# Start addresses of TensorE's operands in a hybrid conformer block: moving tiles and the low halves of the weights shifted within 256 bytes

## The chip, the cores and the metric

The kernel runs on one core of a Trainium2 chip. The metric is the device time of one execution in microseconds (us). TensorE (PE in the profile) multiplies, VectorE (DVE), ScalarE (ACT) and GpSimd (POOL) work on vectors, and SyncE (SP) issues the DMAs. PEld is the row of TensorE's weight loads.

## The reference

Two layers over 256 tokens of width 2048, all in float32. Layer 0 mixes by a convolution branch and a pooling branch, layer 1 by a short gated convolution, and each layer ends in a SwiGLU of width 5632:

```python
for i in range(2):
    h = h + (conv_pool_mixer if i == 0 else short_conv_mixer)(h, ...)
    h = h + swiglu(rms_norm(h, ffn_norm[i]), w_gate[i], w_up[i], w_down[i])
return rms_norm(h, final_norm)

def swiglu(h, w_gate, w_up, w_down):
    return (silu(h @ w_gate) * (h @ w_up)) @ w_down

def short_conv_mixer(x, norm_g, w_in, conv_w, w_out):
    gate_b, gate_c, v = split(rms_norm(x, norm_g) @ w_in, 3)
    return (gate_b * causal_depthwise_conv(gate_c * v, conv_w)) @ w_out
```

The weights are some 390 MB, and each 128x128 block of them is used once, against 256 tokens.

## The kernel before

**Blocks and halves.** All weights lie in one array `wall` as a sequence of 128x128 blocks, in the order in which TensorE uses them. `fetch` (lines 100 to 104) brings them in units of 16 blocks (1 MB). `prepare` (106 to 122) takes a piece of 8 blocks: ScalarE rounds it to float32r into the tile `hi` (line 114), and VectorE, or GpSimd for some early pieces, writes the remainder `w - hi` to the tile `lo` (line 121). There are 6 buffers of each, and pieces are prepared 4 ahead.

**Moving operands.** The activations are split in the same way. Per 128 features, a moving tile holds 256 columns of the high part and then 256 columns of the low part, together 2048 bytes in each partition. There are four such tiles. `xs` (line 210) is the normed input of every stage, `cat` (373) the output of the two branches of the first mixer, `y` (541) the gated product of a SwiGLU half, and `z` (566) the gated convolution of the second mixer.

**Three products for one block.** `product` (161 to 168) has two forms. The narrow one, used in the first mixer and for the last 22 blocks, issues three matmuls of 256 columns: `hi` by the high part (166), `hi` by the low part (167), `lo` by the high part (168). The wide one, used everywhere else, issues two: `hi` by all 512 columns (163), and `lo` by the 256 columns of the high part (164). Each matmul brings its own load of a 128x128 weight tile. In the trace this load begins together with the matmul ahead of the one that it belongs to. Columns of one matmul are therefore read while the next weights are read.

**Stages, in order.** The first mixer (called m0) runs from the start to about 260 us. The first SwiGLU follows, in two halves: gate and up by `xs` (704 blocks), and down by `y` (352 blocks). Then comes the second mixer (m1: 768 blocks by `xs`, 256 by `z`) and the second SwiGLU, like the first. The order on each engine is set when the program is built. Matmuls in a stage follow block by block; VectorE's and ScalarE's work is placed between them by `tick`, by dependencies and by the free buffers.

**Addresses.** The program gives every tile a fixed start in the partition. Buffers of `hi` and `lo` are 4096 bytes apart, blocks in a piece 512 bytes apart, and chunks of a moving tile 2048 bytes apart. So a tile keeps one start modulo 256 for all its blocks. In the kernel before, `hi`, `lo` and `xs` all start at 64 modulo 256, `cat` at 96, and `y` and `z` at 160.

Of the kernel before, what the change touches and what calls it, by code (L numbers as in the profile page):

```python
# [12 lines left out]
F32R = mybir.dt.float32r  # L13
# [4 lines left out]
P = 128  # L18
T = 256
D = 2048  # L20
NC = D // P
DC = 1024
NA = DC // P
FF = 5632
NF = FF // P
NH = NF // 2
# [38 lines left out]
UNIT_AT = [sum(UNITS[:u]) for u in range(len(UNITS))]  # L65

PIECE = 8
PIECES = [(u, o, min(PIECE, n - o)) for u, n in enumerate(UNITS) for o in range(0, n, PIECE)]

LOOK = 4  # L70
AHEAD = 1

WARM = 9

KEEP = 8

POOL_SPLIT = range(96, 24 * NC + 16 + 7 * NC + 8)

# [6 lines left out]
def block_kernel(ctx: ExitStack, tc: tile.TileContext, xT: bass.AP, xtok: bass.AP, vec: bass.AP, wall: bass.AP, out: bass.AP):  # L85
    nc = tc.nc
    const = ctx.enter_context(tc.tile_pool(name="const", bufs=1))
    act = ctx.enter_context(tc.tile_pool(name="act", bufs=1))
    wst = ctx.enter_context(tc.tile_pool(name="wst", bufs=4))
    whl = ctx.enter_context(tc.tile_pool(name="whl", bufs=6))  # L90
# [9 lines left out]
    def fetch(u):  # L100
        if u < len(UNITS) and u not in loaded:
            n, off = UNITS[u], UNIT_AT[u] * P * P
            loaded[u] = w = wst.tile([P, 16 * P], F32, name="w")
            nc.sync.dma_start(w[:, : n * P], wall[off : off + n * P * P].rearrange("(p f) -> p f", p=P))  # L104

    def prepare(i):
        if i >= len(PIECES) or i in ready:
            return
        u, o, n = PIECES[i]
        fetch(u)  # L110
        w = loaded[u][:, o * P : (o + n) * P]
        hi = whl.tile([P, PIECE * P], F32R, name="hi")
        lo = whl.tile([P, PIECE * P], F32R, name="lo")
        nc.scalar.copy(hi[:, : n * P], w)  # L114
        engine = nc.vector
        if UNIT_AT[u] + o in POOL_SPLIT:
            if relief:
                relief.pop()
            else:
                engine = nc.gpsimd  # L120
        engine.tensor_tensor(out=lo[:, : n * P], in0=w, in1=hi[:, : n * P], op=ALU.subtract)  # L121
        ready[i] = (hi, lo)

    def next_block():
        b, i = cursor
        at = UNIT_AT[PIECES[i][0]] + PIECES[i][1]
        if b == at + PIECES[i][2]:
            ready.pop(i)
            i, at = i + 1, b
        for j in range(i, i + LOOK + 1):  # L130
            prepare(j)
        if i + LOOK < len(PIECES):
            for u in range(PIECES[i + LOOK][0] + 1, PIECES[i + LOOK][0] + AHEAD + 1):
                fetch(u)
        cursor[:] = [b + 1, i]
        hi, lo = ready[i]
        o = (b - at) * P
        return hi[:, o : o + P], lo[:, o : o + P]
# [8 lines left out]
    def tick():  # L147
        for name, q in queues.items():
            credit[name] = credit[name] + 1.0 if q else 0.0
            while q and credit[name] >= PACE[q[0][0]]:  # L150
                cost, step = q.popleft()
                credit[name] -= PACE[cost]
                step()
# [7 lines left out]
    def product(acc, hi, lo, x, first, last, wide):  # L161
        if wide:
            nc.tensor.matmul(acc, hi, x, start=first, stop=False, skip_group_check=True)  # L163
            nc.tensor.matmul(acc[:, T:], lo, x[:, :T], start=False, stop=last, skip_group_check=True)  # L164
        else:
            nc.tensor.matmul(acc[:, :T], hi, x[:, :T], start=first, stop=False)  # L166
            nc.tensor.matmul(acc[:, :T], hi, x[:, T:], start=False, stop=False)  # L167
            nc.tensor.matmul(acc[:, :T], lo, x[:, :T], start=False, stop=last)  # L168

    def matmul_chunks(xs, ks, n=1, wide=False, behind=None):  # L170


        accs = [ps.tile([P, 2 * T], F32, name="acc") for _ in range(n)]
        for i, k in enumerate(ks):
            first, last = i == 0, i == len(ks) - 1
            for acc in accs:
                hi, lo = next_block()
                product(acc, hi, lo, xs[:, k, :], first, last, wide)
                tick()
            if behind is not None:  # L180
                behind(k)
        return accs
# [10 lines left out]
    def split(dst, src, scale=None):  # L193

        if scale is None:
            nc.scalar.copy(dst[:, :T], src)
            nc.vector.tensor_tensor(out=dst[:, T:], in0=src, in1=dst[:, :T], op=ALU.subtract)
        else:
            nc.scalar.activation(dst[:, :T], src, AF.Copy, scale=scale)
            nc.vector.scalar_tensor_tensor(out=dst[:, T:], in0=src, scalar=scale, in1=dst[:, :T], op0=ALU.mult, op1=ALU.subtract)  # L200
# [4 lines left out]
    def col(name, i):  # L205
        return v[:, VECS[name] + i : VECS[name] + i + 1]

    identity = v[:, VECS["identity"] :]
    h = act.tile([P, NC, T], F32, name="h")
    xs = act.tile([P, NC, 2 * T], F32R, name="xs")  # L210
    ones = const.tile([P, P], F32, name="ones")
    nc.gpsimd.memset(ones, 1.0)

# [14 lines left out]
    def rsqrt_of(*totals, scale, halves=False, st=None):  # L228
# [9 lines left out]
        if halves:  # L238

            idle = ps.tile([P, P], F32, name="idle", tag="acc")  # L240
            with tc.issue_after(mm.ins):
                for _ in range(KEEP):
                    nc.tensor.matmul(idle, ones, ones, start=True, stop=True)  # L243
# [27 lines left out]
    class Norm:  # L271


        def __init__(self, gain, final=False):
            self.gain, self.final = gain, final
            self.sums = []

        def add(self, c):
# [6 lines left out]

        def scale(self, c):
            if not self.final:
                split(xs[:, c, :], h[:, c, :], col(self.gain, c))

        def square(self, c):  # L290
            if c == 0:
# [37 lines left out]
        return s  # L329


    norm = Norm("mix_norm_e")
    nc.sync.dma_start(v[:, :NC], vec[:, :NC])

    def load(at, n):
# [30 lines left out]
    every = range(NC)  # L366
    with tc.tile_pool(name="m0", bufs=1) as m0, tc.tile_pool(name="ps_side", bufs=2, space=PSUM) as ps_side:
# [1 line left out]
        a_in = m0.tile([P, NA, pad + T], F32, name="a_in")  # L369
        nc.gpsimd.memset(a_in[:, :, :pad], 0.0)  # L370
        conv = m0.tile([P, NA, T], F32, name="conv")
        cat = m0.tile([P, NA, 2 * T], F32R, name="cat")
        total = m0.tile([P, 2, T], F32, name="total")

        sides, prods, state = {}, {}, {}
# [156 lines left out]

        project(xs, POOL_CHUNKS)
        drain()
        norm = Norm("ffn_norm0")
        project(cat, range(NA), norm)

    def swiglu(norm, following):
        with tc.tile_pool(name="ffn", bufs=1) as fp:
            phase[0] = fp  # L540
            y = fp.tile([P, NH, 2 * T], F32R, name="y")
            r = None
            for half in range(2):
                for f in range(NH):
                    (acc_g,) = matmul_chunks(xs, every, wide=True)
                    (acc_u,) = matmul_chunks(xs, every, wide=True)
                    if r is None:
                        r = norm.rstd()
                    gate = scaled(acc_g, r, "gate", True)
                    up = scaled(acc_u, r, "val", True)  # L550
                    nc.scalar.activation(gate, gate, AF.Silu)
                    nc.vector.tensor_tensor(out=up, in0=up, in1=gate, op=ALU.mult)
                    split(y[:, f, :], up)
                project(y, range(NH), following if half else None, wide=True, narrow_end=half and following.final)
# [1 line left out]
    x0.close()  # L556


    after = Norm("mix_norm_o")
    swiglu(norm, after)  # L560


    norm = Norm("ffn_norm1")
    with tc.tile_pool(name="m1", bufs=1) as m1:
        phase[0] = m1
        z = m1.tile([P, NC, 2 * T], F32R, name="z")
        pad = SW - 1
        r = None
        for c in range(NC):
            (acc_c,) = matmul_chunks(xs, every, wide=True)  # L570
            (acc_v,) = matmul_chunks(xs, every, wide=True)
            if r is None:
                r = after.rstd()
            cg = scaled(acc_c, r, "gate", True)
            vv = scaled(acc_v, r, "val", True)
            cv = m1.tile([P, pad + T], F32, name="cv", bufs=2)
            nc.gpsimd.memset(cv[:, :pad], 0.0)
            nc.vector.tensor_tensor(out=cv[:, pad:], in0=cg, in1=vv, op=ALU.mult)
            wc = VECS["conv_w_o"] + c * SW
            co = m1.tile([P, T], F32, name="co", bufs=2)  # L580
            nc.vector.tensor_scalar(out=co, in0=cv[:, :T], scalar1=v[:, wc : wc + 1], scalar2=None, op0=ALU.mult)
            for k in range(1, SW):
                nc.vector.scalar_tensor_tensor(out=co, in0=cv[:, k : k + T], scalar=v[:, wc + k : wc + k + 1], in1=co, op0=ALU.mult, op1=ALU.add)
            (acc_b,) = matmul_chunks(xs, every, wide=True)
            bg = scaled(acc_b, r, "pv", True)
            nc.vector.tensor_tensor(out=bg, in0=bg, in1=co, op=ALU.mult)
            split(z[:, c, :], bg)
        project(z, every, norm, wide=True)


    last = Norm("final_norm", final=True)
    swiglu(norm, last)
    halves = rsqrt_of(*last.sums, scale=1.0 / D, halves=True)
    with tc.tile_pool(name="fin", bufs=1) as fin:

# [90 lines left out]
```

## Time and profile before

| | us |
|---|---|
| median of 3 runs (lowest, highest) | 2105.78 (2104.46, 2109.65) |
| the profiled execution | 2103.73 |
| its span, first to last instruction | 2102.0 |
| bytes read from HBM | 391.39 MB, 187 GB/s over the span |

The page gives each engine's busy time, the chain of work that ended last, and groups of instructions by source line with the mean duration of one. How fast matmuls follow each other isn't in these groups, since they overlap in the pipeline: the mean of one wide `hi` matmul is 391 ns, though they and their `lo` matmuls take turns. That rate comes from another view, the instructions of one source line in a window of time: it prints how many there are and when the first and the last began. The time between the two, divided by the count less one, is the time from one block to the next.

### The profile page before, as it was taken

Reading aid. Unit: us, or ns where it says so; the run is one execution under the profiler, and the core shown is the slowest. Engines: PE = TensorE matmul, PEld = TensorE weight load, DVE = VectorE, ACT = ScalarE, POOL = GpSimd, SP = SyncE. Lnnn points to the kernel's source line nnn. Section 1 sums busy time; section 2 is a strip of 40 time slices with the busy share of each in tenths; the row PEclk is TensorE's granted clock in tenths of the full one; section 3 lists DMA queues with packets and bytes.
Section 4 is the critical chain, followed back from the end, with each engine's and each line's share of the span. In section 5 each row is a group of like instructions: output and inputs, shape, how many; then the busy total and the mean of one; then the engine's idle time right before and its main releaser. Section 6 shows DMA issues by size and latency. Waiting matters only on the chain.

```text
span 2102.0 us, 31608 instructions
## 1 busy us (share of the span) xinstructions
PE 2079.1 (99%) x12584; PEld 1855.8 (88%) x12584; DVE 1383.4 (66%) x1979; ACT 1060.9 (50%) x1571; POOL 200.6 (10%) x180
## 2 busy tenths in 40 slices
PE   8999999999999999999999999999999999999998
PEld 8999988888888888888888888888888888888887
DVE  6888866666556666666777777666666556666654
ACT  7776654444444444454444445554444444444453
POOL 3985200000000000011000001100000000000011
PEclk9999999999999999999999999999999999999999
DMA  8554455555555555555555555555555555555551
GB/s 326 187 191 168 158 184 197 183 198 182 194 185 188 193 187 194 183 196 182 183 198 182 198 183 193 180 189 198 183 196 184 189 192 183 198 182 199 182 192 68
DMA packets 56884, 395.53 MB, mean 188 GB/s; under 512 B 6432, under 2 KB 7200, under 8 KB 9760
## 3 DMA queue, kind: packets, MB, share of 16 engines
q1 hardware_dynamic: 56736, 393.52, 52.4%
q8 instruction: 98, 1.61, 0.3%
q14 instruction: 50, 0.41, 0.1%
HBM read 391.39 MB, written 2.10 MB: 187 GB/s over the span
## 4 chain that ended last, share of the span: by engine, by line
PE 98%; DMA 1%; DVE 1%; ACT 0%; SPq 0%; issue 0%; DVEq 0%; ACTq 0%
PE acc L163 57%; PE acc L164 30%; PE acc L166 4%; PE acc L168 4%; PE acc L167 4%; DMA rows<-in_xtok 0%; DMA h<-in_xT 0%; DVE res L603 0%; ACT hi L114 0%; PE st L237 0%; PE st L268 0%; DVE lo L121 0%; SPq L104 0%; ACT conv L475 0%; PE idle L243 0%
## 5 line engine op out<-in xcount | busy, mean ns | idle before, releaser
L114 ACT CAST hi<-w 128x1024 fp32r<-128x1024 f32 (+1 forms) x740 | 776.1, 1050 | 975.3 <-PE acc L163 621.0
L121 DVE TENSOR_TENSOR lo<-w,hi 128x1024 fp32r<-128x1024 f32 (+1 forms) x691 | 845.2, 1224 | 639.5 <-ACT hi L114 635.3
L163 PE MATMUL acc<-xs,hi 128*128 128x512 f32 x3584 | 1243.3, 391 | 0.0
L164 PE MATMUL acc<-xs,lo 128*128 128x256 f32 x3584 | 1004.7, 280 | 0.0
L163 PEld LDWEIGHTS acc<-xs,hi 128*128 128x128 f32 x3584 | 670.4, 187 | 146.2
L164 PEld LDWEIGHTS acc<-xs,lo 128*128 128x128 f32 x3584 | 678.1, 189 | 0.1
L163 PE MATMUL acc<-y,hi 128*128 128x512 f32 x1386 | 485.2, 393 | 0.0
L164 PE MATMUL acc<-y,lo 128*128 128x256 f32 x1386 | 386.4, 279 | 0.0
L163 PEld LDWEIGHTS acc<-y,hi 128*128 128x128 f32 x1386 | 259.4, 187 | 61.7
L164 PEld LDWEIGHTS acc<-y,lo 128*128 128x128 f32 x1386 | 259.9, 187 | 0.4
L298 POOL TENSOR_TENSOR sumsq<-sumsq,sq 128x256 f32<-128x256 f32 x56 | 58.8, 1050 | 1599.1 <-ACT sq L296 1599.1
L166 PE MATMUL acc<-xs,hi 128*128 128x256 f32 x512 | 144.0, 284 | 5.2 <-ACT hi L114 4.2
L167 PE MATMUL acc<-xs,hi 128*128 128x256 f32 x512 | 143.6, 283 | 0.0
L168 PE MATMUL acc<-xs,lo 128*128 128x256 f32 x512 | 141.3, 284 | 0.1
L121 POOL TENSOR_TENSOR lo<-w,hi 128x1024 fp32r<-128x1024 f32 x49 | 118.7, 2441 | 43.1 <-PE acc L167 34.3
L166 PEld LDWEIGHTS acc<-xs,hi 128*128 128x128 f32 x512 | 98.1, 192 | 6.2 <-ACT hi L114 5.0
L167 PEld LDWEIGHTS acc<-xs,hi 128*128 128x128 f32 x512 | 98.2, 192 | 0.0
L168 PEld LDWEIGHTS acc<-xs,lo 128*128 128x128 f32 x512 | 96.5, 192 | 0.5 <-DVE lo L121 0.5
L163 PE MATMUL acc<-z,hi 128*128 128x512 f32 x256 | 89.6, 393 | 0.0
L188 ACT COPY cross<-acc 128x256 f32<-128x256 f32 x224 | 80.6, 360 | 0.0
L164 PE MATMUL acc<-z,lo 128*128 128x256 f32 x256 | 71.3, 279 | 0.0
L318 DVE TENSOR_TENSOR h<-acc,h 128x256 f32<-128x256 f32 x112 | 47.2, 423 | 18.9 <-PE acc L168 13.2
(134 smaller groups left out, 1198.6 us busy)
## 6 DMA issues: line engine op xcount, KB each, us to landing
w<-in_wall SPq DMA_DIRECT2D x365, 1024.0 KB, 4.8
w<-in_wall SPq DMA_DIRECT2D x7, 512.0 KB, 7.7
rows<-in_xtok SPq DMA_DIRECT2D x2, 1024.0 KB, 7.9
h<-in_xT SPq DMA_DIRECT2D x7, 256.0 KB, 7.3
out<-res SPq DMA_DIRECT2D x2, 512.0 KB, 2.8
out<-res SPq DMA_DIRECT2D x2, 384.0 KB, 2.8
v<-in_vec SPq DMA_DIRECT2D x1, 260.0 KB, 6.7
h<-in_xT SPq DMA_DIRECT2D x2, 128.0 KB, 2.3
```

The lines of the kernel that those rows point to most:

```text
L114: nc.scalar.copy(hi[:, : n * P], w)
L121: engine.tensor_tensor(out=lo[:, : n * P], in0=w, in1=hi[:, : n * P], op=ALU.subtract)
L163: nc.tensor.matmul(acc, hi, x, start=first, stop=False, skip_group_check=True)
L164: nc.tensor.matmul(acc[:, T:], lo, x[:, :T], start=False, stop=last, skip_group_check=True)
L166: nc.tensor.matmul(acc[:, :T], hi, x[:, :T], start=first, stop=False)
L167: nc.tensor.matmul(acc[:, :T], hi, x[:, T:], start=False, stop=False)
L168: nc.tensor.matmul(acc[:, :T], lo, x[:, :T], start=False, stop=last)
L188: nc.scalar.copy(t, acc[:, T:])
L298: nc.gpsimd.tensor_tensor(out=self.sums[0], in0=self.sums[0], in1=sq, op=ALU.add)
L318: nc.vector.tensor_tensor(out=h[:, n, :], in0=acc[:, :T], in1=h[:, n, :], op=ALU.add)
```

## The change

No instruction is added, removed or moved: on each of the five engines, the instructions stand in the same order with the same shapes as before. What differs is where the operands lie.

- `xs` gets 256 bytes more room, and each norm writes and reads it through a view that begins `at` bytes in: 32 for m0, 160 for all later stages. `y` and `z` get 128 bytes more, and begin 64 bytes in. `cat` stays where it was (offset 0).
- Each `lo` buffer gets 512 bytes more, and its view begins 0 bytes in for m0, then 32, 64, 96, 128 and 192 bytes in, from part to part. The shift grows at the block numbers in `LO_AT`. The `hi` buffers keep their place modulo 256.

In the table, "by" is the moving operand's start less the weights' start, modulo 256 bytes.

| part (blocks) | moving | before: by `hi` / by `lo` | after: by `hi` / by `lo` |
|---|---|---|---|
| m0, narrow (512) | xs | 0 / 0 | 32 / 32 |
| m0, narrow (144) | cat | 32 / 32 | 32 / 32 |
| first SwiGLU, half 1 (704, 352) | xs, y | 0 / 0, 96 / 96 | 160 / 128 |
| first SwiGLU, half 2 (704, 352) | xs, y | 0 / 0, 96 / 96 | 160 / 96 |
| m1 (768, 256) | xs, z | 0 / 0, 96 / 96 | 160 / 64 |
| second SwiGLU, half 1 (704, 352) | xs, y | 0 / 0, 96 / 96 | 160 / 32 |
| second SwiGLU, half 2 (704, 330 and 22 narrow) | xs, y | 0 / 0, 96 / 96 | 160 / 224 |

The core of the diff:

```diff
+_m0, _ffn = 24 * NC + 16 + NC * NC, 3 * NH * NC
+LO_AT = {_m0: 32, _m0 + _ffn: 32, _m0 + 2 * _ffn: 32, _m0 + 2 * _ffn + 64 * NC: 32, _m0 + 3 * _ffn + 64 * NC: 64}
+XS_M0 = 32
+XS_F0 = 160
+XS_M1 = 160
+XS_F1 = 160
+Y_F0 = 64
+Y_F1 = 64
+Z_M1 = 64
+CAT = 0
...
-        lo = whl.tile([P, PIECE * P], F32R, name="lo")
+        lo = whl.tile([P, PIECE * P + 128], F32R, name="lo")
+        at = sum(LO_AT[b] for b in LO_AT if b <= UNIT_AT[u] + o) // 4
+        lo = lo[:, at : at + PIECE * P]
...
-    xs = act.tile([P, NC, 2 * T], F32R, name="xs")
+    xs_room = act.tile([P, NC * 2 * T + 64], F32R, name="xs")
+    def moving(room, at, n):
+        return room[:, at // 4 : at // 4 + n * 2 * T].rearrange("p (c t) -> p c t", c=n)
...
-        def __init__(self, gain, final=False):
+        def __init__(self, gain, at=0, final=False):
             self.gain, self.final = gain, final
+            self.xs = moving(xs_room, at, NC)
...
-                split(xs[:, c, :], h[:, c, :], col(self.gain, c))
+                split(self.xs[:, c, :], h[:, c, :], col(self.gain, c))
...
-        cat = m0.tile([P, NA, 2 * T], F32R, name="cat")
+        cat = moving(m0.tile([P, NA * 2 * T + 32], F32R, name="cat"), CAT, NA)
...
-            y = fp.tile([P, NH, 2 * T], F32R, name="y")
+            y = moving(fp.tile([P, NH * 2 * T + 32], F32R, name="y"), at, NH)
...
-        z = m1.tile([P, NC, 2 * T], F32R, name="z")
+        z = moving(m1.tile([P, NC * 2 * T + 32], F32R, name="z"), Z_M1, NC)
```

More of the change, by code (lines that the diff above doesn't have):

```diff
@@ L329, in scaled @@
         return s
-    norm = Norm("mix_norm_e")
+    norm = Norm("mix_norm_e", XS_M0)
+    xs = norm.xs
     nc.sync.dma_start(v[:, :NC], vec[:, :NC])
@@ L534, in block_kernel, with swiglu @@
         drain()
-        norm = Norm("ffn_norm0")
+        norm = Norm("ffn_norm0", XS_F0)
         project(cat, range(NA), norm)
-    def swiglu(norm, following):
+    def swiglu(norm, following, at):
         with tc.tile_pool(name="ffn", bufs=1) as fp:
             phase[0] = fp
-            y = fp.tile([P, NH, 2 * T], F32R, name="y")
+            y = moving(fp.tile([P, NH * 2 * T + 32], F32R, name="y"), at, NH)
             r = None
@@ L544, in swiglu @@
                 for f in range(NH):
-                    (acc_g,) = matmul_chunks(xs, every, wide=True)
-                    (acc_u,) = matmul_chunks(xs, every, wide=True)
+                    (acc_g,) = matmul_chunks(norm.xs, every, wide=True)
+                    (acc_u,) = matmul_chunks(norm.xs, every, wide=True)
                     if r is None:
@@ L556, in block_kernel @@
     x0.close()
-    after = Norm("mix_norm_o")
-    swiglu(norm, after)
-    norm = Norm("ffn_norm1")
+    after = Norm("mix_norm_o", XS_M1)
+    swiglu(norm, after, Y_F0)
+    norm = Norm("ffn_norm1", XS_F1)
     with tc.tile_pool(name="m1", bufs=1) as m1:
         phase[0] = m1
-        z = m1.tile([P, NC, 2 * T], F32R, name="z")
+        z = moving(m1.tile([P, NC * 2 * T + 32], F32R, name="z"), Z_M1, NC)
         pad = SW - 1
@@ L569, in block_kernel @@
         for c in range(NC):
-            (acc_c,) = matmul_chunks(xs, every, wide=True)
-            (acc_v,) = matmul_chunks(xs, every, wide=True)
+            (acc_c,) = matmul_chunks(after.xs, every, wide=True)
+            (acc_v,) = matmul_chunks(after.xs, every, wide=True)
             if r is None:
@@ L583, in block_kernel @@
                 nc.vector.scalar_tensor_tensor(out=co, in0=cv[:, k : k + T], scalar=v[:, wc + k : wc + k + 1], in1=co, op0=ALU.mult, op1=ALU.add)
-            (acc_b,) = matmul_chunks(xs, every, wide=True)
+            (acc_b,) = matmul_chunks(after.xs, every, wide=True)
             bg = scaled(acc_b, r, "pv", True)
@@ L591, in block_kernel @@
     last = Norm("final_norm", final=True)
-    swiglu(norm, last)
+    swiglu(norm, last, Y_F1)
     halves = rsqrt_of(*last.sums, scale=1.0 / D, halves=True)
```

## The prediction

> **What bounds the kernel now.** I read the page first, from the busy times to the chain that ended last.
>
> ```profile
> span 2102.0 us, 31608 instructions
> PE 2079.1 (99%) x12584; PEld 1855.8 (88%) x12584; DVE 1383.4 (66%) x1979; ACT 1060.9 (50%) x1571; POOL 200.6 (10%) x180
> ...
> PEclk9999999999999999999999999999999999999999
> DMA  8554455555555555555555555555555555555551
> ...
> PE 98%; DMA 1%; DVE 1%; ACT 0%; SPq 0%; issue 0%; DVEq 0%; ACTq 0%
> ```
>
> TensorE ends 98% of the chain at a full granted clock, while the DMA engines are about half busy. So the time is the number of matmuls by the time from one to the next. The groups by line give the counts:
>
> ```profile
> L163 PE MATMUL acc<-xs,hi 128*128 128x512 f32 x3584 | 1243.3, 391 | 0.0
> L164 PE MATMUL acc<-xs,lo 128*128 128x256 f32 x3584 | 1004.7, 280 | 0.0
> L163 PE MATMUL acc<-y,hi 128*128 128x512 f32 x1386 | 485.2, 393 | 0.0
> L166 PE MATMUL acc<-xs,hi 128*128 128x256 f32 x512 | 144.0, 284 | 5.2 <-ACT hi L114 4.2
> L163 PE MATMUL acc<-z,hi 128*128 128x512 f32 x256 | 89.6, 393 | 0.0
> ```
>
> There are 3584 wide blocks by xs and 1386 + 256 = 1642 wide blocks by y or z, none with idle time ahead. 512 narrow blocks go by xs, with 5.2 us of waits. The means overlap and aren't prices. The time from block to block is in the view of one line in a window: xs wide in two windows, y, z, and then xs narrow in m0, xs being at distance 0 and y and z at 96.
>
> ```profile
> L163 PE MATMUL acc<-xs,hi x578: 390/391/392, 299.7 to 499.7; 128*128 128x512 f32 x193
> ...
> L163 PE MATMUL acc<-xs,hi x434: 390/391/392, 1099.8 to 1249.9; 128*128 128x512 f32 x145
> ...
> L163 PE MATMUL acc<-y,hi x321: 392/394/397, 506.0 to 618.0; 128*128 128x512 f32 x161
> ...
> L163 PE MATMUL acc<-z,hi x250: 392/393/397, 1264.8 to 1352.0; 128*128 128x512 f32 x125
> ...
> L168 PE MATMUL acc<-xs,lo x167: 283/283/284, 60.0 to 119.7; 128*128 128x256 f32 x167
> ```
>
> By division: xs wide 200.0/577 = **346.6 ns** a block, in the second window 150.1/433 = 346.7. y takes 112.0/320 = **350.0**, z 87.2/249 = 350.2, and xs narrow 59.7/166 = **359.6**. All three forms stream 768 columns a block (512 + 256, or 3 x 256), yet they differ. For the narrow form the first mixer holds a comparison that counts here: `cat` is at distance 32, where xs is at 0. The three lines of its last stretch, and the narrow blocks of y at the very end (distance 96):
>
> ```profile
> L166 PE MATMUL acc<-cat,hi x113: 277/280/281, 218.8 to 258.8; 128*128 128x256 f32 x113
> ...
> L167 PE MATMUL acc<-cat,hi x116: 277/279/281, 218.9 to 258.9; 128*128 128x256 f32 x116
> ...
> L168 PE MATMUL acc<-cat,lo x116: 277/280/281, 219.0 to 258.7; 128*128 128x256 f32 x116
> ...
> L168 PE MATMUL acc<-y,lo x22: 278/280/283, 2081.2 to 2088.7; 128*128 128x256 f32 x22
> ```
>
> 113 + 116 + 116 = 345 matmuls begin between 218.8 and 258.9, which is 40.1/344 = 116.6 ns each or **350 ns** a block. Narrow y takes 7.5/21 = 357. The durations say the same: 277 to 281 ns by cat, 283 to 284 by xs. Is it the load on other engines? These windows answer; their columns are the busy times of PE, PEld, DVE, ACT and POOL:
>
> ```profile
> 0.00:25.00 25.00, 19.77 (x141) 18.75 (x142) 13.19 (x24) 17.06 (x29) 1.71 (x36) 1.00 0.89 333
> 25.00:100.00 75.00, 74.00 (x613) 73.50 (x613) 63.11 (x118) 59.59 (x99) 59.73 (x32) 1.00 0.64 237
> ...
> 300.00:500.00 200.00, 200.00 (x1156) 176.49 (x1155) 129.32 (x180) 96.78 (x145) 0.00 (x0) 1.00 0.54 190
> 1100.00:1250.00 150.00, 150.00 (x867) 132.39 (x866) 108.74 (x163) 66.99 (x91) 0.79 (x8) 1.00 0.54 190
> ```
>
> DVE is busy 65% of the one wide window and 72% of the other, and the block takes 346.6 and 346.7 ns. POOL is busy 80% of the time in the narrow window from 25 us, and nearly idle at the end, where narrow y is still slow. So I read the differences as the operands' places: moving columns and the next weights are read together, and how the reads meet sets the pace.
>
> **The floor.** What would a block cost if nothing met? Four rows of the timeline at 300 us (start, duration):
>
> ```profile
> 300.01 0.39 PE L163 MATMUL acc<-xs,hi 128*128 128x512 f32 x1
> 300.24 0.28 PE L164 MATMUL acc<-xs,lo 128*128 128x256 f32 x1
> 300.35 0.39 PE L163 MATMUL acc<-xs,hi 128*128 128x512 f32 x1
> 300.58 0.28 PE L164 MATMUL acc<-xs,lo 128*128 128x256 f32 x1
> ```
>
> The lo matmul follows its hi matmul after 230 ns, and the next hi matmul follows after the rest of the block, 346.6 - 230 = 116.6. The 256 columns by which the two differ thus cost 113.4 ns, and 768 columns at that rate are **340 ns**. Above this floor lie 6.6 ns in an xs block, 10.1 in a y or z block, 19.6 in a narrow xs block and 10 in a cat block.
>
> [...]
>
> **The change part by part.**
>
> *Narrow xs, from 0 to 32.* This is the one step that the trace prices directly, since cat stands at 32 / 32 already: 359.6 to 350, 9.6 ns a block. Of the 512 blocks, some 41 (123 matmuls, the 141 of the first window less 18 warm-up ones) run while the first loads arrive, and what they save is waited. The other 471 save 4.5 us. The cover that must hold is VectorE and ScalarE in m0; VectorE is busy 63 of 75 us there, so there is room. One place could take part of it back, the wait ahead of the last product of m0:
>
> ```profile
> 205.93 0.13 PE acc L167
> ...
> 206.14 1.05 ACT hi L114
> 207.22 1.23 DVE lo L121
> ...
> 208.99 0.89 PE st L268 x2
> 209.90 0.70 DVE conv L473
> 210.62 2.07 ACT conv L475 x4
> ```
>
> The chain of waits enters this stretch from a PE matmul at 205.93, so an earlier PE brings it forward. I take 4.5, with bounds of 0 (the vector work is late instead) and 471 x 19.6 = 9.2 (down to the floor).
>
> *Wide xs, from 0 / 0 to 160 / 128, 96, 64, 32 and 224.* No row stands at 160. The bounds are the floor (a gain of 3584 x 6.6 = 23.7 us) and, on the other side, the slowest pace that 768 columns show, 359.6 (a loss of 3584 x 13 = 46.6). I go by the nearest row, cat at 32: 160 is 32 plus half of 256, and if banks repeat after 128 bytes, it is the same place. There the excess over the floor is half of what it is at distance 0 (10 of 19.6). Half of 6.6 is 3.3 a block: 3584 x 3.3 = **11.8 us** gained, at 343.3 ns.
>
> *Wide y and z, from 96 / 96 to the same distances.* They stream like xs, so I give them the same 343.3 ns: 1642 x 6.8 = **11.2 us**. Bounds: 16.6 to the floor, and a loss of 15.8 at 359.6.
>
> *The low halves' shifts.* They set which place of lo's weights meets the 512 columns. One part has 96, where y and z are slow with both halves, and one has 32. Apart from the hi halves no row shows any of them, so they are inside the bounds above and I add nothing. The 22 narrow blocks of y at 160 / 224 are worth 22 x 10 ns = 0.2 us either way, left out.
>
> *Addresses on the other engines.* ScalarE and VectorE write xs, y, z and lo a little further on, in the same order and shapes. A piece of 8 blocks takes 8 x 343.3 = 2.75 us on TensorE, and its conversions are these:
>
> ```profile
> L114 ACT CAST hi<-w 128x1024 fp32r<-128x1024 f32 (+1 forms) x740 | 776.1, 1050 | 975.3 <-PE acc L163 621.0
> L121 DVE TENSOR_TENSOR lo<-w,hi 128x1024 fp32r<-128x1024 f32 (+1 forms) x691 | 845.2, 1224 | 639.5 <-ACT hi L114 635.3
> w<-in_wall SPq DMA_DIRECT2D x365, 1024.0 KB, 4.8
> ```
>
> 1.05 and 1.22 us of 2.75, mostly waiting for TensorE to free buffers. Weights must come at 1 MB in 16 x 343.3 ns = 5.5 us, 191 GB/s where the windows show 190 at half the DMA engines' time. Nothing becomes late. I cost this at zero; if either conversion were over 2.75 us, it would set the pace.
>
> **Sum.** 4.5 + 11.8 + 11.2 = 27.5 us off the profiled execution's 2103.7, giving 2076.2. The median of the runs is 2.1 us above the profiled one, so the forecast is **2078 us**.
>
> **The rivals.**
>
> *Wide blocks don't care for 160 any more than for 0* (chance 0.16). xs stays at 346.6, y and z come down to it (1642 x 3.5 = 5.7), narrow xs gains its 4.5: 10.2 off, **2096**. For it: xs holds 346.6 in every window, a steady meeting that a shift may leave as it is. Against it: y at 96 is slower, so distance matters to wide blocks too.
>
> *All the way to the floor* (0.13): 23.7 + 16.6 + 9.2 = 49.5 off, **2056**. For it: the excess is only what meets, and 160 / 96 and so on keep moving columns and weights apart from the start. Against it: no stretch of the trace goes at 340.
>
> *Nothing changes* (0.12, with small effects that cancel): TensorE's two reads don't meet, and the paces come from something else in each stage, such as the order in which buffers come free: **2106**. Against it stand the even load in the windows, and narrow xs and cat with the same lines and shapes in neighbouring stages. [...]
>
> *Slower: 160 is 96 seen from the other end* (0.17). 256 - 160 = 96, so if what matters is how near two reads are in either order, xs goes from its good place to that of y. It would take 350 ns: 3584 x 3.4 = 12.2 us more, y and z unchanged, 4.5 off in m0: 7.7 more, **2114**. The place is every wide block by xs, most clearly lines 163 and 164 from 300 to 500 us. It decides from a block time of 346.6 + 10.2/3584 us = 349.4 ns for xs, where y and z stay at 350. For it: y and z at 96 are the only wide rows off 0, and they are slower, as is narrow y.
>
> **How the numbers follow.** The forecast has 0.42, the floor 0.13, the partial case 0.16, no change 0.12 and the slower case 0.17. About 0.3%, or 6 us, is what a measurement of this kernel can tell from no change. The forecast, the floor and the partial case are faster by more: 0.71. No change is 0.12, slower 0.17. The range reaches from just under the floor to the slower case, 2053 to 2114, which leaves out some steps below the floor and what lies beyond 350 ns a block. Forecast alone: 2065 to 2090, for a half that may be a quarter or three quarters.
>
> **What would show it.** In the profile after, the same views: line 163's successor by xs from 300 us should step at about 343 ns a block, y and z the same, narrow xs in m0 at 350. The part with the best low half will show by comparing 704 blocks of xs in each SwiGLU half; if the low half doesn't matter, all five agree. The prediction is wrong if wide xs steps at 346 or more, if the parts differ by more than the halving (then the low halves decide, and not the moving place), or if idle time appears ahead of line 163.

## The result, and the profile after

| | before | after |
|---|---|---|
| median of 17 runs each, us | 2105.13 | 2110.38 |
| lowest to highest, us | 2104.09 to 2110.85 | 2108.9 to 2111.91 |
| span of the profiled execution, us | 2102.0 | 2107.1 |

The ratio of after to before is 1.0022, with a 95% interval of 1.0014 to 1.0029. The change makes the kernel about 5 us slower, where 27 us of gain were forecast. The first lines of the page after (span; busy time, share and count of each engine; the engines in the chain that ended last):

```profile
span 2107.1 us, 31608 instructions
...
PE 2085.8 (99%) x12584; PEld 1853.6 (88%) x12584; DVE 1383.8 (66%) x1979; ACT 1060.9 (50%) x1571; POOL 200.4 (10%) x180
...
PE 98%; DMA 1%; DVE 1%; ACT 0%; SPq 0%; issue 0%; DVEq 0%; ACTq 0%
```

Only TensorE moved: PE is busy 6.7 us longer, the other engines' busy times are as before within 0.4 us (PEld, which PE covers, is 2.2 us shorter), and PE still ends 98% of the chain. So the answer is again in the time from block to block. In the changed kernel lines 178 and 179 are the wide form, 181 to 183 the narrow one. First the narrow blocks of m0 and the start of the wide ones, then the five wide parts, `xs` ahead of `y` or `z` (count, durations, first and last start):

```profile
L183 PE MATMUL acc<-xs,lo x170: 277/280/281, 59.7 to 118.9; 128*128 128x256 f32 x170
...
L178 PE MATMUL acc<-xs,hi x69: 390/396/477, 254.8 to 280.0; 128*128 128x512 f32 x69
...
L178 PE MATMUL acc<-xs,hi x629: 392/393/397, 279.6 to 499.8; 128*128 128x512 f32 x158
L178 PE MATMUL acc<-y,hi x332: 387/393/397, 509.7 to 625.7; 128*128 128x512 f32 x166
...
L178 PE MATMUL acc<-xs,hi x700: 397/397/398, 626.8 to 873.8; 128*128 128x512 f32 x175
L178 PE MATMUL acc<-y,hi x324: 397/397/398, 884.7 to 998.8; 128*128 128x512 f32 x162
...
L178 PE MATMUL acc<-xs,hi x710: 388/394/398, 1019.7 to 1266.7; 128*128 128x512 f32 x178
L178 PE MATMUL acc<-z,hi x228: 388/394/398, 1277.8 to 1356.9; 128*128 128x512 f32 x114
...
L178 PE MATMUL acc<-xs,hi x642: 394/394/395, 1379.6 to 1604.0; 128*128 128x512 f32 x161
L178 PE MATMUL acc<-y,hi x324: 389/394/397, 1614.8 to 1727.9; 128*128 128x512 f32 x162
...
L178 PE MATMUL acc<-xs,hi x703: 389/389/389, 1728.9 to 1970.0; 128*128 128x512 f32 x176
L178 PE MATMUL acc<-y,hi x302: 391/397/400, 1979.9 to 2085.9; 128*128 128x512 f32 x151
```

Time from first to last over the count less one, in ns a block, beside what it was before:

| part | by hi / by lo | xs: before, after | y or z: before, after |
|---|---|---|---|
| m0, narrow | 32 / 32 | 359.6, 350.3 | |
| first SwiGLU, half 1 | 160 / 128 | 346.6, 350.6 | 350.0, 350.5 |
| half 2 | 160 / 96 | 346.6, 353.4 | 350, 353.3 |
| m1 | 160 / 64 | 346.7, 348.4 | 350.2, 348.5 |
| second SwiGLU, half 1 | 160 / 32 | 346.6, 350.1 | 350, 350.2 |
| half 2 | 160 / 224 | 346.6, **343.4** | 350, 352.2 |

The narrow term came as forecast: the first wide block begins at 254.8 us now, and before at 259.5, by the same view:

```profile
L163 PE MATMUL acc<-xs,hi x56: 391/392/475, 259.5 to 279.9; 128*128 128x512 f32 x56
```

The wide parts by `xs` lose 704 x (4.0 + 6.8 + 3.5 - 3.2) + 768 x 1.7 ns = 9.1 us, those by `y` and `z` about 1.7, which with -4.7 gives +6 against the 5.1 of the spans. In all the wide parts the moving operand stands at 160 by `hi`, yet their paces run from 343.4 to 353.4. What differs from part to part is the place of the low halves.

### The profile page after: what moved, and what is told of

Read it like the earlier page. It is cut to its first block, busy times and chain, and to the rows that moved or that the text cites. A ratio compares the mean times of both kernels' runs of the same rounds, so it can differ in the third digit from the quotient of the medians.

```text
span 2107.1 us, 31608 instructions
## 1 busy us (share of the span) xinstructions
PE 2085.8 (99%) x12584; PEld 1853.6 (88%) x12584; DVE 1383.8 (66%) x1979; ACT 1060.9 (50%) x1571; POOL 200.4 (10%) x180
## 4 chain that ended last, share of the span: by engine, by line
PE 98%; DMA 1%; DVE 1%; ACT 0%; SPq 0%; issue 0%; DVEq 0%; ACTq 0%
PE acc L178 57%; PE acc L179 29%; PE acc L181 4%; PE acc L183 3%; PE acc L182 3%; DMA rows<-in_xtok 0%; DMA h<-in_xT 0%; DVE res L625 0%; ACT hi L129 0%; PE st L257 0%; DVE lo L136 0%; PE st L288 0%; SPq L117 0%; ACT conv L497 0%; ACT rows L371 0%; PE idle L263 0%
```

## The experiments

Three theories were put against each other. **M**: the moving operand's place sets the pace, and 160 is 96 seen from the other end. **L**: the low halves' places do the harm. **P**: the pair of distances decides, and neither of the two alone. A fourth came up on the way, that what ran before counts as well (**path**). A pair is written as the distance by `hi` / by `lo`. A pace below is worked out from first and last start as above, or, for short stretches, from the starts of the blocks in the trace, over the second half of the stretch.

### The narrow part alone

```diff
-LO_AT = {_m0: 32, ...}
+LO_AT = {}
-XS_F0 = 160      (XS_M1, XS_F1 the same; Y_F0, Y_F1, Z_M1 from 64 to 0)
+XS_F0 = 0
```

> Only the narrow part of the change: xs 32 bytes on in m0, every wide part at the old distances (0 / 0 for xs, 96 / 96 for y and z). If the first term of the prediction holds, m0 ends 4.7 us earlier (as in the changed kernel, 254.8 instead of 259.5 us) and nothing else moves: about 2100.5 against 2105.1, a ratio of 0.998. If a gain in m0 is lost again in later waits: 2105. Wide xs should go on at 346.7 ns a block.

Measured: 2100.98 us against 2105.2, ratio 0.998 (0.9971 to 0.9989). Wide xs in the window of the prediction's first row:

```profile
L178 PE MATMUL acc<-xs,hi x578: 391/391/391, 299.7 to 499.7; 128*128 128x512 f32 x193
```

It goes on at 346.6, as before. So the narrow term is worth 4.2 us by the medians. In this kernel's trace the time from the 41st narrow block to the 512th is 169.9 us, where it was 174.2. But the first wide block begins at 256.5 us and not at the 254.8 expected: part of the gain went again in the stretch between, which takes 60.7 us here, 59.4 in the kernel before and 59.9 in the changed one. Why it differs is open. The loss of the change lies in its wide parts, and amounts to 2110.38 - 2100.98 = 9.4 us there.

### The moving place alone

```diff
-LO_AT = {_m0: 32, _m0 + _ffn: 32, _m0 + 2 * _ffn: 32, ...}
+LO_AT = {}
```

> The moving places of the change (160, narrow 32) with the low halves not shifted: 160 / 160 in all wide parts. Theory M (the moving place alone sets the pace, and 160 is 96 seen from the other end): xs at 350 ns a block, y and z at 350, time 2105 - 4.7 + 12.2 = 2112 to 2113. Theory L (the low halves' places did the harm, 160 itself is good): xs, y and z near the 343.4 ns that the changed kernel shows in its one fast part, 2105 - 4.7 - 11.8 - 11.0 = 2077 to 2078. Theory P (the pair of distances, with hi by moving and lo by moving, decides): one pace in all wide parts, not told by the runs so far, between 340 and 354 ns.

Measured: **2095.24 us**, ratio 0.9952 (0.9939 to 0.9966). Line 178 in three parts, xs, y and z:

```profile
L178 PE MATMUL acc<-xs,hi x702: 391/392/392, 624.7 to 867.7; 128*128 128x512 f32 x176
...
L178 PE MATMUL acc<-y,hi x318: 391/392/392, 879.8 to 989.7; 128*128 128x512 f32 x159
...
L178 PE MATMUL acc<-z,hi x234: 391/392/400, 1264.9 to 1345.7; 128*128 128x512 f32 x117
```

243.0/701 = 346.6 for xs, 109.9/317 = 346.7 for y and 80.8/233 = 346.8 for z. So 160 / 160 has the pace of 0 / 0 for all three. M falls (350 was due), and L in its strong form (343.4) too. y and z gain 3.4 ns a block, 5.6 us, and m0 its 4.2, together 9.8 of the 10.0 measured. The changed kernel differs from this one in the low halves' shifts alone, with the same room for every tile, so these shifts cost 2110.38 - 2095.24 = **15.1 us**.

### The low halves alone

```diff
-XS_M0 = 32
+XS_M0 = 0
-XS_F0 = 160      (XS_M1, XS_F1 the same; Y_F0, Y_F1, Z_M1 from 64 to 0)
+XS_F0 = 0
```

> The low halves' shifts alone: hi at 0 for xs and 96 for y and z as before, lo by xs at 224, 192, 160, 128 and 64 from part to part, by y and z 64, 32, 0, 224 and 160. Theory M: all parts of xs at 346.7, y and z at 350, time 2105. Theory L: the first part's xs (lo at 224) at 343.4 as in the changed kernel's last part, the last part's (lo at 64) near 348.4, since lo alone decides. Theory P: neither; paces that differ from part to part and don't repeat those of the changed kernel at the same lo distance.

Measured: 2112.27 us, ratio 1.0033 (1.0018 to 1.0047). xs in the five parts, lo at 224, 192, 160, 128 and 64:

```profile
L178 PE MATMUL acc<-xs,hi x649: 389/396/398, 280.2 to 504.9; 128*128 128x512 f32 x163
...
L178 PE MATMUL acc<-xs,hi x699: 391/392/393, 631.0 to 872.9; 128*128 128x512 f32 x175
...
L178 PE MATMUL acc<-xs,hi x722: 392/396/400, 1011.9 to 1265.8; 128*128 128x512 f32 x181
...
L178 PE MATMUL acc<-xs,hi x657: 392/393/400, 1372.8 to 1602.8; 128*128 128x512 f32 x165
...
L178 PE MATMUL acc<-xs,hi x701: 392/394/397, 1726.7 to 1971.7; 128*128 128x512 f32 x176
```

That is 346.8, 346.6, 352.1, 350.6 and 350.0 (the third and fourth windows hold a few stalls; without them 351.7 and 350.0). At 0 / 224 xs takes 346.8 where 160 / 224 took 343.4, and at 0 / 160 it takes 351.7 where 160 / 160 took 346.6. The lo distance alone doesn't tell the pace, and at one hi distance the paces run from 346.6 to 351.7: P. These are single pairs, and some of them have a second pace (0 / 160 has 347 in one place of the map below), so the maps weigh more.

### A map of the pairs, with the kernel around it and without

Each of the two kernels ran once. The first shifts `hi` and `lo` of each piece so that all 64 pairs in steps of 32 bytes come by:

```diff
+        at_hi, at_lo = (-by % 256 // 4 for by in BY[UNIT_AT[u] + o])
+        hi = hi[:, at_hi : at_hi + PIECE * P]
+        lo = lo[:, at_lo : at_lo + PIECE * P]
```

> A map: moving tiles as before, but hi and lo of each piece are shifted so that every pair of distances by hi and by lo in steps of 32 bytes (64 pairs) holds for 48 wide blocks by xs, 38 of them again in another order by y and z, and 8 equal and 6 unequal pairs for 24 narrow blocks each. Theory M: rows of the map (one hi distance) are constant, 346.7 at 0, 350 at 96 and 160. Theory L: columns (one lo distance) are constant, 343.4 at 224 and about 353 at 96. Theory P: neither rows nor columns are constant, and the same pair gives the same pace for y and z as for xs. If paces also depend on what ran before (the changed kernel's last y part goes from 343 to 352 ns within a part), some pairs differ by several ns between their two places. Narrow: 360 ns at 0, 350 at 32, 360 at 96. As a whole near 2105 +- 10.

The second runs TensorE alone. It leaves out everything else that the block computes: the tiles are filled once, and no weights are fetched or converted while it multiplies. One chain is a sum of 16 blocks.

```diff
+    for d, e in GRID + AGAIN:
+        chains(d, e, 3)
+    for d, e in SMALL:
+        chains(d, e, 3, 32)
```

> TensorE alone: no conversions, no vector work and no loads of weights during the matmuls; hi, lo and the moving tile are filled once. It runs the 64 pairs of distances for 48 wide blocks each, then the 64 pairs again in another order, then six pairs with weights of 32 columns instead of 128. The output is zeros. If what meets is TensorE's own reads (theory P), the paces are those of the map, 340 at 64 / 0 and 347 to 353 elsewhere, with no other engine at work. If other engines' or the DMA's reads and writes make the excess, all pairs go at one pace, at or below 340. If the meeting is with the load of the next weights, 32 columns of weights bring every pair down to 340 or under.

The page of the second kernel shows that no other engine works beside TensorE:

```profile
span 2259.8 us, 25783 instructions
...
PE 2249.4 (100%) x12864; PEld 1944.2 (86%) x12864; ACT 10.6 (0%) x7; POOL 3.7 (0%) x5
```

Its paces in ns a block, rows by the distance by `hi`, columns by `lo`. Two numbers stand where the pair's two places in the program differ by 1 ns or more (at the first place of 0 / 0, where the program starts, a break in the order of the matmuls is left out):

| hi \ lo | 0 | 32 | 64 | 96 | 128 | 160 | 192 | 224 |
|---|---|---|---|---|---|---|---|---|
| 0 | 353 | 353 | 351, 350 | 347, 351 | 347, 350 | 347, 352 | 347 | 347 |
| 32 | 344 | 347 | 353 | 347, 353 | 349 | 347 | 347 | 349 |
| 64 | **340** | 349 | 353 | 349 | 347 | 349 | 347 | 347 |
| 96 | 349 | 347 | 353 | 350 | 347 | 353 | 349 | 347, 350 |
| 128 | 352 | 347 | 347 | 351 | 351 | 352 | 347 | 351 |
| 160 | 350, 347 | 350 | 353, 348 | 353 | 351 | 347 | 348, 353 | 352 |
| 192 | 350, **340** | 351 | 353 | 347 | 353 | 353 | 353 | 347, 351 |
| 224 | 351 | 350, 347 | 351 | 351 | 353 | 350 | 348, 351 | 353 |

Three things are in it. No row and no column is constant (P). The kernel around hardly matters: in 62 of the 64 pairs the first map has xs within 0.5 ns of a pace found here, though there DVE, ACT and the DMAs are at work (the other two hold a stall), and the 37 pairs that y and z run there lie within 2 ns of one. And 13 pairs have two paces (path). Where they do, the durations differ as well. This is 192 / 0 in the second kernel, at its first and its second place:

```profile
L115 PE MATMUL acc<-xs,hi x48: 393/396/402, 815.0 to 831.5; 128*128 128x512 f32 x48
...
L115 PE MATMUL acc<-xs,hi x48: 389/389/390, 1890.9 to 1906.9; 128*128 128x512 f32 x48
```

The same addresses modulo 256, 396 ns and 389 ns at the median. The mean of the first numbers is 349.5, so a pair drawn blindly is on average slower than the 346.7 that xs had at 0 / 0 in the kernel before. The table doesn't hold every pace: that 346.7 at 0 / 0 and the 343.4 at 160 / 224, which whole kernels keep for hundreds of blocks, aren't in it.

The narrow form has paces of its own. In the first map it takes 360 ns at 0 / 0, 350 at 32 / 32 and 360 at 96 / 96, as expected, and 340 at 192 / 192, where the wide form takes 353.

Weights of 32 columns bring 160 / 96 and 192 / 192 from 353 to 347, but 64 / 0 from 340 up to 347. The expectation that a shorter load brings every pair to 340 or under fails. The paces do change with the width of the weights; but such a block also writes 32 rows of the sum instead of 128, so this doesn't show that the load is what counts, nor which reads meet where.

### One pair everywhere

```diff
-LO_AT = {_m0: 32, _m0 + _ffn: 32, _m0 + 2 * _ffn: 32, ...}
+LO_AT = {_m0: 192}
```

> The change with one shift of the low halves for all wide parts, 192 bytes, so 160 by hi and 224 by lo as in the changed kernel's last part, where xs went at 343.3 ns and y fell from 343 to 352 at its second chain, as two hi matmuls stood behind each other. Theory P alone: one pace in all parts, 343.3 by xs, y and z: 2105 - 4.7 - 12 - 11 = 2077. Path: xs at 343.3 in some parts and near 352 in others, and y and z start at 343 and leave it for 352 where the order of hi and lo matmuls is broken; with xs at 343.3 and y and z at 352: 2105 - 4.7 - 12 + 3 = 2091.

Measured: 2105.23 us, ratio 0.9993 (0.9983 to 1.0003). xs and y of the first SwiGLU, and then xs and y of its second half, all at 160 / 224:

```profile
L178 PE MATMUL acc<-xs,hi x640: 391/397/400, 279.8 to 504.8; 128*128 128x512 f32 x160
...
L178 PE MATMUL acc<-y,hi x323: 389/389/392, 515.3 to 625.9; 128*128 128x512 f32 x162
...
L178 PE MATMUL acc<-xs,hi x703: 389/389/389, 626.9 to 867.9; 128*128 128x512 f32 x176
...
L178 PE MATMUL acc<-y,hi x322: 391/397/400, 877.9 to 990.9; 128*128 128x512 f32 x161
```

225.0/639 = 352.1, then 110.6/322 = 343.5, 241.0/702 = 343.3 and 113.0/321 = 352.0. One pair, two steady paces, in turns, and each holds for hundreds of blocks. xs is at the slow one in three of its five parts, so the whole gains nothing and comes out above both numbers expected. Where they switch shows in the timeline. This is the changed kernel near the start of its last y part (start, duration; "x2" are two matmuls in one row):

```profile
1977.85 0.39 PE L178 MATMUL acc<-y,hi 128*128 128x512 f32 x1
1978.07 0.28 PE L179 MATMUL acc<-y,lo 128*128 128x256 f32 x1
1978.19 0.39 PE L178 MATMUL acc<-y,hi 128*128 128x512 f32 x1
...
1978.88 0.62 PE L178 MATMUL acc<-y,hi 128*128 128x512 f32 x2
1979.34 0.40 PE L179 MATMUL acc<-y,lo 128*128 128x256 f32 x2
1979.57 0.40 PE L178 MATMUL acc<-y,hi 128*128 128x512 f32 x1
1979.81 0.28 PE L179 MATMUL acc<-y,lo 128*128 128x256 f32 x1
1979.92 0.40 PE L178 MATMUL acc<-y,hi 128*128 128x512 f32 x1
```

Up to 1978.88 blocks follow after 0.34 us (343 ns). There two `hi` matmuls stand together and then two `lo` matmuls. 26 blocks stand ahead of the second `hi`, which fits the last of a sum's 22 blocks standing behind the fifth of the next sum (21 + 5). Behind it blocks take 0.35 us and more, and the part never returns. In the kernel of this experiment the pace of y switches at the same spot in all four of its parts (514, 877, 1611 and 1974 us), twice to the faster and twice to the slower one. The part by z has the same break and stays at 352 on both sides of it, so a break doesn't always switch. That it is the break that switches y is read from the trace; no run was made without it.

The two paces are two rhythms. In this kernel's trace the blocks at the fast pace take, from start to start, 345 and 342 ns in turn (at times 341), those at the slow one 354, 357, 344, 352 and 353, and again from the front. A rhythm of five blocks fits neither the 8 blocks of a piece nor the 16 or 22 of a sum, so it is hardly the address of a single block that makes it. That each block depends on how the ones ahead of it fell is the author's reading; no run shows it directly.

### The fastest pair in the whole kernel

```diff
-LO_AT = {_m0: 32, _m0 + _ffn: 32, ...}
+LO_AT = {_m0: 64}
-XS_M0 = 32
+XS_M0 = 192
-XS_F0 = 160      (XS_M1, XS_F1 the same)
+XS_F0 = 64
-Y_F0 = 64        (Y_F1, Z_M1 the same)
+Y_F0 = 224
-CAT = 0
+CAT = 160          (lo, cat, y, z with the room for it)
```

> All wide parts at 64 by hi and 0 by lo, all narrow ones at 192 / 192, the fastest pairs of the map (340.0 and 340.3 ns a block there). If a pair keeps its pace when a whole kernel runs at it (theory P): wide xs from 346.7 to 340, y and z from 350.1 to 340, narrow xs from 360 to 340.3, which is 23.9 + 16.6 + 9.2 = 49.7 us off 2105.2, about 2055 to 2056. Theory L in its form that lo alone decides: lo at 0 for xs is where the kernel before has it, so 346.7 in wide parts, and only m0 and y and z gain: 2105 - 9 - 5.7 = 2090. If what ran before decides more than the pair does (path): paces between 340 and 350, 2056 to 2100, that differ between parts with the same pair.

Measured: **2056.77 us** (2053.62 to 2059.6), ratio 0.9764 (0.975 to 0.9777), faster than both kernels. The groups of the page, then xs wide, y, and narrow xs in an early and a late stretch of m0:

```profile
L178 PE MATMUL acc<-xs,hi 128*128 128x512 f32 x3584 | 1220.0, 389 | 0.0
L179 PE MATMUL acc<-xs,lo 128*128 128x256 f32 x3584 | 990.1, 276 | 0.0
...
L178 PE MATMUL acc<-xs,hi x701: 389/389/389, 616.9 to 854.9; 128*128 128x512 f32 x176
...
L178 PE MATMUL acc<-y,hi x310: 389/389/389, 509.8 to 614.9; 128*128 128x512 f32 x155
...
L183 PE MATMUL acc<-xs,lo x168: 281/281/281, 59.8 to 118.8; 128*128 128x256 f32 x168
...
L183 PE MATMUL acc<-xs,lo x98: 276/276/276, 158.0 to 190.9; 128*128 128x256 f32 x98
```

238.0/700 = **340.0** for xs and 105.1/309 = 340.1 for y: the floor of the prediction, held in every wide part, on both sides of the break too. The narrow pair has two paces here, 59.0/167 = 353.3 early and 32.9/97 = 339.2 late (the window cuts a few reordered blocks; most take 340 from start to start in the trace). So the narrow term didn't come as expected: the first wide block begins at 255.3 us, 4.2 us earlier than before, not 9.2. The profiled execution is the slowest of the five, 2059.6 us. Its span is 2057.8, 44.2 shorter than before, which the wide parts (3584 x 6.6 + 1642 x 10.1 ns = 40.2 us) and the 4.2 of m0 account for. The median is 49.3 us under the 2106.1 of the kernel before in the same session, as much as was expected, but where the faster executions gained the rest is in no trace.

### Around the fastest pair

TensorE alone again, the same kernel with other pairs, run once; the output is again left out:

```diff
-    for d, e in GRID + AGAIN:
+    for d, e in FINE:                      # 40 to 88 by hi, 232 to 24 by lo, in steps of 8
+        chains(d, e, 3)
+    for d, e in BEFORE:                    # six other pairs, each followed by 64 / 0
+        chains(d, e, 2)
+        chains(64, 0, 2)
```

> TensorE alone again, around the fastest pair, 64 by hi and 0 by lo: 49 pairs in steps of 8 bytes (40 to 88 by 232 to 24), 48 blocks each; then 64 / 0 entered from six other pairs; then 64 / 0 with hi, lo or both 256 bytes further, and 192 / 0; then four pairs with weights of 64 columns. The output is zeros. If only the place modulo 256 counts, the three pairs 256 further go at 340 as well; if 512 counts, some don't. If 64 / 0 is a steady pace whatever ran before, all six entries come to 340 within their 32 blocks; if it is one of two paces, as with 160 / 224, some stay near 347 to 352. If reads meet in lines of 32 bytes, all pairs whose places fall in the same lines go at 340; if single words count, only 64 / 0 does.

The fine map is as rugged as the coarse one. 64 / 240, 88 / 240 and 88 / 0 reach 340, while 56 / 0 has 346.7, 64 / 8 has 353.3 and 72 / 0 has 348.3. Steps of 8 bytes go with other paces, which speaks against lines of 32 bytes as the unit: 64 / 8, 64 / 16 and 64 / 24 have 353, 347 and 350. Each pair ran once there, though, and with two paces possible it isn't shown pair by pair. With hi, lo or both 256 bytes further, 64 / 0 keeps its 340 in all three cases. Entered from six other pairs it comes to 340 five times, and once, from 192 / 192, stays at 349.9; in the fine part, entered from 64 / 248, it has 350.0. So the fastest pair has a second pace as well, though every wide part of the whole kernel found the first. With weights of 64 columns 64 / 0 and 0 / 0 take 340, 192 / 192 and 32 / 0 take 347.

## Why the prediction was wrong

**The frame held.** TensorE sets the time (98% of the chain that ended last, before and after), the order is untouched, no conversion or load became late (0.0 us of idle time ahead of the wide `hi` matmuls on both pages), and operands' places move the pace by some per cent (340 to 353 ns a wide block in the map).

**The narrow term was right**: 4.5 us forecast, 4.2 measured alone; 350.3 ns a block against 350. It rested on a row of cat at the very pair and in the same narrow form.

**The wide term of xs failed** at the step "160 is 32 plus half of 256, and if banks repeat after 128 bytes, it is the same place". At 160 / 160 xs has 346.7 instead of 343.3, the very pace of 0 / 0. The halving behind it was taken over from the narrow form, and that fails even without the period: wide blocks at 32 / 32 take 346.7 as well. Narrow and wide paces don't go together at all, as 192 / 192 shows with 340 narrow and 353 wide. That there are banks which repeat was an assumption: no run shows any, nor does the map show a period of 128, as 32 / 0 and 160 / 0 have 344 and 350 or 347. The 343.4 that the last part did reach, at 160 / 224, is luck: the same pair also holds 352.

**For y and z** half of the term was right, 350 to 346.7 instead of 343.3 with the moving place alone, which is the rival "wide blocks don't care": 2096 forecast for it, 2095.2 measured.

**The low halves' shifts were costed at nothing**, and this is the step that turned the forecast gain into a loss: "Apart from the hi halves no row shows any of them, so they are inside the bounds above and I add nothing." They cost 15.1 us. Without them the change gains 10.0. The bounds did hold this loss, but zero was no middle of them. The paces of 64 pairs have a mean of 349.5, and xs stood at 346.7, already one of the better ones: a blind shift of the low halves was more likely to lose than to gain.

**The slower rival** named the place and nearly the price, xs wide at 350, 2114 against 2110.4, but its reason fell: 160 / 160 isn't 96 / 96. The floor rival's 340 ns is real, but at another pair; the kernel at 64 / 0 comes to its price, 2056.8 against 2056, though the narrow half of that price isn't seen in the trace.

**The rival of no change** looked for the cause of the paces outside the operands, such as in the order in which buffers come free. Its price, 2106, came within 4.4 us of the result, but that cause fails: with TensorE alone the same work takes 340 to 353 ns by its own operands' addresses, and with the other engines at work 62 of the 64 pairs keep a pace found there within 0.5 ns. Whether TensorE's two reads hold each other up is not shown.

Still open: why these pairs and not others, and what makes one pair hold two rhythms. That moving columns and the next weights meet was the prediction's reading; the runs show that addresses move the pace and that they do so with TensorE alone (340 to 353 ns), but not that this meeting is how. Weights of 32 columns bring two pairs down from 353 to 347 and 64 / 0 up to it from 340, so a plain account of columns that meet weights in one line isn't enough.

## What to carry to other kernels

Where TensorE streams without idle time, look at the time from one matmul to the next of a line, not at the mean duration, and compare stages whose operands start at other addresses. Here a pair of start addresses is worth up to 4% of the matmuls' time (340 against 353 ns a block), and it isn't to be had by a rule from one distance: move one operand at a time, measure all pairs in one run, in the form in which the kernel uses them, and then see whether the pair holds its pace in the whole kernel. 48 blocks a pair found the fastest one here, but missed the second paces of others. A shift whose price no row shows should be costed at the mean of what such places cost, where that is known, and not at nothing.

## What the runs showed that was not expected

The pace of matmuls depended on the path: at 160 / 224 it was 343 or 352 ns a block over hundreds of blocks at the same start addresses modulo 256, at 192 / 0 it was 350 or 340, and at 64 / 0, with TensorE alone, 340 after five other pairs and 349.9 after 192 / 192. At 160 / 224 the two paces were rhythms of two and of five blocks (345 and 342 ns in turn; 354, 357, 344, 352 and 353). No pair went below 340 ns for 768 columns, with TensorE alone as in the whole kernel.
